# Low parts of weight chunks on a second engine in the mixer's input projection of a decoder step

## The chip, the cores and the metric

The kernel runs on one core of one Trainium2 chip. The metric is the device time of one launch in microseconds (us), the median of several runs. The engines are called by the profile's names: PE (TensorE, matrix products), DVE (VectorE), ACT (ScalarE), POOL (GpSimd) and SP (SyncE, which here only issues DMAs). SBUF is the on-chip memory that all of them read; PE writes its products to PSUM, from where DVE and ACT read them.

## The reference

One layer of a hybrid decoder is computed for 256 new prompt tokens and 8 sample tokens (264 columns in all), with 2048 features. Everything is fp32.

```
x = x + 0.5 * swiglu(rmsnorm(x, n1), f1g, f1u, f1d)          # FFN 1, inner width 5504
h = rmsnorm(x, nm);  proj = h @ w_in                          # 38 column tiles of 128
o_att  = attend(q, k, v, sinks)                               # sliding window, T5 bias, sinks
o_rwkv, shift, S = rwkv_time_mix(proj[..., ATT_COLS:], ...)   # 16 heads, matrix state 64 x 64
x = x + concat(o_att, o_rwkv) @ w_out
x = x + 0.5 * swiglu(rmsnorm(x, n2), f2g, f2u, f2d)          # FFN 2
y = rmsnorm(x, final_norm)
```

In the recurrence `S = S * exp(lw) + sa * (kk*a) + v * k` the state passes from token to token. The outputs are y, the new key and value windows, the new states S and the shift state (`shift`, the last token's projected columns, which the next step mixes in).

## The kernel before

**Weight products.** A weight matrix comes from HBM in chunks of four 128x128 blocks (128x512 elements). `chunk` loads one (`raw`, six buffers, issued by SP), ACT rounds it to the format that PE takes at full speed (`hi`, L132), and DVE subtracts the two for the rest (`lo`, the low part, L59 through the helper `tt`). `hi` and `lo` have four buffers each. `gemm` then makes three products of 128x264 for each block: hi with the activation's high part, hi with its low part, and lo with its high part, twelve for a chunk. They add up in a PSUM bank `acc`. A tile of the input projection (`win(t)`) takes four chunks.

**Stages.** FFN 1, the mixer, FFN 2. In both FFNs nearly all work is weight products. The mixer goes through 38 input tiles in this order: two tiles for the small projections (t = 0, 1), then four batches of two head pairs, three tiles for each pair (t = 2 to 25), four key and value tiles (26 to 29) and eight query tiles (30 to 37); then the output projection in three passes (`wout`).

**What runs beside it.** Each head pair spawns a task `prep` (decay, keys, products inside blocks of 64 tokens, `gm` and `bk` among its tiles, small `XD` vectors for the sample tokens); each batch spawns one `chain`: it solves a triangular system by 30 dependent steps on DVE (`st`, `Xt`, from L59), builds the transition products (`m<-kr,TT` on PE), copies them out of PSUM (`W` at L622, `uv` at L626), and carries the state through four blocks. `shifted` evicts a tile (`pj`), and POOL copies the last columns into `shc` (L412), the shift state. Query tiles spawn `attend`. The function `tick` advances every task by one step after each chunk, so that small matmuls lie between weight products.

**Order.** The program is written in this interleaved order, and the tile framework's scheduler then lays each engine's instructions down in an order of its own, by priorities and its own model of durations; `tc.high_priority()` marks chunks and evictions. On the chip each engine takes its own queue in order. The queue matters for what follows: an instruction that waits holds all behind it. DMA issues of ACT and SP stand in these queues too, so a store that waits for its data holds the casts behind it.

## Time and profile before

| | |
|---|---|
| median of 3 runs | 1959.75 us (1958.75 to 1960.01) |
| profiled execution | 1958.83 us |
| its span, first to last instruction | 1957.0 us |
| busy PE, PEld | 1940.1, 1922.1 us |
| busy DVE, ACT, POOL | 1313.1, 1036.4, 264.1 us |
| mean granted clock of PE | 0.998 |

The page lists busy time by engine. PEld is the loading of weights into PE, which overlaps its products. A busy PE is not PE at its peak: the ends of matmuls are modelled. The chain of waits goes back from the last instruction to whatever released each step, and so tells which engine set the pace at which time. A row of a timeline has the start in us, the duration in us, the engine, the line, the operation, output and inputs by tile names, shapes, and in brackets the idle time before it and who ended it. A row of the groups by line has the number of instructions (x), their busy us, the mean ns of one, and the idle us ahead of them by releaser. A row of busy time by stretch has the stretch, its length, busy us (and instructions) of PE, PEld, DVE, ACT and POOL, the granted clock, the DMA engines' busy share and GB/s.

### The profile page before, as it was taken

The page shows a single profiled execution, that of the slowest core. Times are in us where ns is not written, and L with a number is a line of the kernel's source. Part 1 is how long each engine was busy: PE and PEld are TensorE (multiplying, and loading weights), DVE is VectorE, ACT ScalarE, POOL GpSimd, SP SyncE. Part 2 cuts the span into 40 slices and gives each one's busy share as a digit, 9 for nine tenths or more (in the row PEclk, how much of TensorE's full clock was granted, in tenths as well). Part 3 has the DMA queues.
Part 4 walks back from the last instruction along what each step waited for, and adds up shares of the span by engine and source line. Part 5 has one row for each costly group of instructions (what it writes and reads, how often), then busy time and mean ns, then how long its engine had stood idle before and what let it go on. Part 6 is the DMA issues. An engine that isn't in the chain of part 4 may idle for free.

```text
span 1957.0 us, 45229 instructions
## 1 busy us (share of the span) xinstructions
PE 1940.1 (99%) x17011; PEld 1922.1 (98%) x17011; DVE 1313.1 (67%) x2591; ACT 1036.4 (53%) x2069; POOL 264.1 (13%) x382
## 2 busy tenths in 40 slices
PE   9999999999999999999999999999999999999998
PEld 9999999999999999999889999999999999999998
DVE  5865555655556567799988766766666666666665
ACT  5644444444444456665556755654444444444445
POOL 0401001010010122232210000210101001010012
PEclk9999999999999999999999999999999999999999
DMA  7666666666656567555455455566666666666654
GB/s 241 178 194 194 186 194 196 184 189 178 188 183 185 184 194 230 165 162 153 136 151 167 137 157 185 176 187 188 191 189 193 188 194 191 191 195 183 195 182 148
DMA packets 218875, 357.26 MB, mean 183 GB/s; under 512 B 33552, under 2 KB 72352, under 8 KB 218656
## 3 DMA queue, kind: packets, MB, share of 16 engines
q1 hardware_dynamic: 212144, 345.76, 59.4%
q10 hardware_dynamic: 6512, 8.61, 1.4%
q8 instruction: 133, 2.18, 0.4%
q14 instruction: 86, 0.70, 0.1%
HBM read 346.67 MB, written 9.69 MB: 182 GB/s over the span
## 4 chain that ended last, share of the span: by engine, by line
PE 95%; DVE 3%; DMA 1%; issue 1%; ACT 1%; SPq 0%; DVEq 0%; POOL 0%; ACTq 0%
PE acc L75 87%; PE m L75 7%; DVE lo L59 1%; DVE Xt L59 0%; DVE st L59 0%; DMA Xt<-sa 0%; DMA x<-in_x 0%; DMA raw<-in_win 0%; DVE y L59 0%; SPq L564 0%; DVE gm L59 0%; ACT t L69 0%; DMA sa<-gm 0%; PE m L782 0%; ACT BT L521 0%
## 5 line engine op out<-in xcount | busy, mean ns | idle before, releaser
L59 DVE TENSOR_TENSOR lo<-raw,hi 128x512 fp32r<-128x512 f32 (+1 forms) x1288 | 874.5, 683 | 511.0 <-ACT hi L132 489.8
L132 ACT CAST hi<-raw 128x512 fp32r<-128x512 f32 (+1 forms) x1288 | 777.0, 606 | 822.0 <-PE acc L75 741.5
L75 PE MATMUL acc<-x,hi 128*128 128x264 f32 x5034 | 932.7, 286 | 2.2 <-DVE o L62 1.2
L75 PEld LDWEIGHTS acc<-x,hi 128*128 128x128 f32 x5034 | 781.4, 189 | 5.8 <-ACT hi L132 2.4
L75 PE MATMUL acc<-x,lo 128*128 128x264 f32 x2517 | 719.8, 286 | 0.5 <-DVE lo L59 0.5
L75 PE MATMUL acc<-h,hi 128*128 128x264 f32 x2752 | 495.0, 284 | 0.0
L75 PEld LDWEIGHTS acc<-x,lo 128*128 128x128 f32 x2517 | 475.5, 189 | 2.9 <-DVE lo L59 1.3
L75 PEld LDWEIGHTS acc<-h,hi 128*128 128x128 f32 x2752 | 424.4, 189 | 0.0
L75 PE MATMUL acc<-h,lo 128*128 128x264 f32 x1376 | 387.8, 284 | 0.0
L75 PEld LDWEIGHTS acc<-h,lo 128*128 128x128 f32 x1376 | 259.2, 189 | 0.0
L59 POOL TENSOR_TENSOR t<-t,t 128x264 f32<-128x264 f32 x74 | 80.3, 1085 | 1095.9 <-DVE t L59 949.7
L75 PE MATMUL acc<-y,hi 128*128 128x264 f32 x648 | 122.7, 284 | 0.0
L75 PE MATMUL acc<-o,hi 128*128 128x264 f32 x648 | 120.1, 284 | 0.0
L75 PE MATMUL acc<-kv,hi 128*128 128x264 f32 x582 | 109.2, 284 | 0.0
L75 PEld LDWEIGHTS acc<-y,hi 128*128 128x128 f32 x648 | 101.2, 189 | 0.1
L75 PEld LDWEIGHTS acc<-o,hi 128*128 128x128 f32 x648 | 100.1, 189 | 0.0
L62 DVE SCALAR_TENSOR_TENSOR x<-acc,x 128x264 f32<-128x264 f32 x192 | 81.2, 427 | 24.5 <-PE acc L75 23.6
L75 PE MATMUL acc<-y,lo 128*128 128x264 f32 x324 | 92.0, 284 | 0.0
L75 PE MATMUL acc<-o,lo 128*128 128x264 f32 x324 | 92.0, 284 | 0.0
L75 PEld LDWEIGHTS acc<-kv,hi 128*128 128x128 f32 x582 | 90.0, 189 | 0.0
L59 DVE TENSOR_TENSOR t<-acc,t 128x264 f32<-128x264 f32 x156 | 67.4, 432 | 32.8 <-PE acc L75 32.8
L75 PE MATMUL acc<-kv,lo 128*128 128x264 f32 x291 | 82.7, 284 | 0.0
(280 smaller groups left out, 1534.9 us busy)
## 6 DMA issues: line engine op xcount, KB each, us to landing
raw<-in_gu SPq DMA_DIRECT2D x688, 256.0 KB, 3.4
raw<-in_dn SPq DMA_DIRECT2D x224, 256.0 KB, 2.9
raw<-in_win SPq DMA_DIRECT2D x152, 256.0 KB, 3.4
raw<-in_dn SPq DMA_DIRECT2D x160, 192.0 KB, 2.7
raw<-in_wout SPq DMA_DIRECT2D x64, 256.0 KB, 3.3
xsp<-x ACTq DMA_DIRECT2D x16, 132.0 KB, 3.6
x<-xsp SPq DMA_DIRECT2D x16, 132.0 KB, 4.0
ld<-in_sT SPq DMA_DIRECT2D x16, 128.0 KB, 3.7
```

What stands on the lines that cost most here:

```text
L59: return e.tensor_tensor(out=out, in0=a, in1=b, op=op)
L62: return V.scalar_tensor_tensor(out=out, in0=a, scalar=s, in1=b, op0=op0, op1=op1)
L75: return TE.matmul(out, lhsT, rhs, start=start, stop=stop, **k)
L132: A.copy(hi[:, :w], raw[:, :w])
```

## The change

Four things are changed.

- From input tile 14 on (24 of 38 tiles), the low part of every second chunk of a tile is subtracted on POOL instead of DVE: 48 instructions.
- In `chain`, the copies `W` (two a batch) and `uv` (four a batch) all go to ACT; before, DVE had half of each.
- The sample tokens' values `Ys[k][:, NP:T]` are copied from `XD` by POOL early in `chain`, instead of by ACT near its end (eight copies of 128x8).
- The store of the shift state `shc` is written into the program at the second query tile instead of behind the last batch's tiles.

```
+SHARE = 14
-        def gemm(ps, src, xs, step=None, rng=None, ahead=True, ready=None):
+        def gemm(ps, src, xs, step=None, rng=None, ahead=True, ready=None, share=False):
...
-                hi, lo = ready or chunk(src[:, k0 * P:k1 * P], k1 - k0, V, ahead)
+                hi, lo = ready or chunk(src[:, k0 * P:k1 * P], k1 - k0, G if share and k0 // CH % 2 else V, ahead)
...
-                gemm(ps, I["win"][t], n2.xs, tick)
+                gemm(ps, I["win"][t], n2.xs, tick, share=t >= SHARE)
...
                 Ys = [yb[bt.p0 + k] for k in range(n)]
+                for k in range(n):
+                    G.tensor_copy(Ys[k][:, NP:T], XD[:, 7, bt.p0 + k, :])
...
-                    (A.copy, V.tensor_copy)[k % 2](W[:, k], v[:, 1:4, 0:64])
+                    A.copy(W[:, k], v[:, 1:4, 0:64])
...
-                        (V.tensor_copy, A.copy)[h](uv[HALF[h], :, k, HALF[h]], v[HALF[h], :, 64:128])
+                        A.copy(uv[HALF[h], :, k, HALF[h]], v[HALF[h], :, 64:128])
...
-                    A.copy(Ys[k][:, NP:T], XD[:, 7, bt.p0 + k, :])
...
-                    if len(bat) == len(BATCH):
-                        A.dma_start(O["sh"], shc)
...
                 else:
+                    if i == 1:
+                        A.dma_start(O["sh"], shc)
                     ps = win(LKV + 4 + i)
```

## The prediction

> **What bounds the kernel now.** I read the page first, then the chain of waits, then busy time by stretch.

> ```profile
> span 1957.0 us, 45229 instructions
> PE 1940.1 (99%) x17011; PEld 1922.1 (98%) x17011; DVE 1313.1 (67%) x2591; ACT 1036.4 (53%) x2069; POOL 264.1 (13%) x382
> ...
> 65.80 691.23 PE acc L75 x5760
> ```

> The page makes TensorE (PE) look full everywhere. That is true of the two FFNs: the chain has 5760 weight products in a row, 691.23 / 5760 = 0.120 us each, with nothing between them. One weight chunk is 12 products, so PE needs 12 x 0.120 = 1.44 us for it. In the mixer the same 99% is misleading, because the modelled ends of matmuls cover their gaps. There I go by who leads the chain. The tiles that the change touches (14 to 37) run from the load in the first row below to the eviction of the last query tile in the second.

> ```profile
> 833.42 0.33 SPq L131 DMA_DIRECT2D raw<-in_win  x1
> ...
> 1066.88 0.43 DVE L62 SCALAR_TENSOR_TENSOR o<-acc,rs 128x264 f32<-128x264 f32 x1
> ```

> I cut these 234 us where the chain changes its leader. Busy time of PE, PEld, DVE, ACT, POOL in each piece:

> ```profile
> 833.00:861.00 28.00, 28.00 (x228) 27.70 (x227) 27.56 (x69) 18.78 (x48) 10.48 (x18) 1.00 0.60 182
> 861.00:879.00 18.00, 17.10 (x243) 16.11 (x243) 16.58 (x58) 11.96 (x36) 3.72 (x13) 1.00 0.50 133
> 879.00:932.00 53.00, 53.00 (x591) 50.75 (x584) 48.24 (x123) 32.83 (x74) 10.77 (x22) 1.00 0.54 152
> 932.00:960.00 28.00, 26.16 (x379) 23.88 (x379) 24.07 (x76) 15.69 (x44) 7.43 (x17) 1.00 0.55 150
> 960.00:989.00 29.00, 29.00 (x318) 27.62 (x315) 28.18 (x89) 17.72 (x39) 4.51 (x12) 1.00 0.43 124
> 989.00:1029.00 40.00, 37.47 (x545) 35.26 (x545) 31.11 (x93) 21.07 (x57) 6.18 (x16) 1.00 0.55 148
> 833.00:1067.00 234.00, 228.46 (x2647) 216.93 (x2647) 208.01 (x606) 142.00 (x358) 47.34 (x104) 1.00 0.53 150
> ```

> The chain's shares by line, first for 879 to 932, then for 989 to 1029, then for the whole 833 to 1067:

> ```profile
> by line: PE acc L75 73.4%; PE m L75 25.7%; PE m L474 1.1%
> by line: DVE lo L59 13.7%; PE acc L75 12.1%; DMA raw<-in_win 10.0%; DVE st L59 9.1%; DVE Xt L59 8.9%; issue 7.3%; SPq L564 5.9%; DMA Xt<-sa 5.5%; DVE t L442 4.3%; DMA sa<-gm 3.8%; DVE o L62 2.5%; DVE t L59 1.9%; DVE kr L59 1.6%; DVE uv L626
> by line: PE acc L75 49.6%; PE m L75 15.2%; DVE lo L59 5.0%; DVE Xt L59 3.5%; DVE st L59 3.4%; issue 3.2%; DMA Xt<-sa 2.7%; DMA raw<-in_win 1.7%; SPq L564 1.5%; DVE gm L59 1.4%; DMA sa<-gm 1.0%; ACT BT L521 0.9%; DVE t L59 0.8%; ACT kr L512
> ```

> So PE leads some pieces wholly (100% in 879 to 932) and others hardly at all (12.1% in 989 to 1029). Over the whole, 64.8% is PE; about a third of 234 us, some 80 us, is led by something else, and VectorE (DVE) is most of that. DVE is busy 208.01 of 234 us, and in the PE-led pieces before each gap it is at 91 to 98%, so its backlog is carried into the next gap. DVE work taken out of a PE-led piece therefore still counts, one piece later. That holds until 1029; behind it PE leads again, and I give relief there no value.

> **The parts, one by one.** Groups by line, DVE and ACT; the first three rows are for 833 to 1067, the others for 757 to 1205:

> ```profile
> L59 DVE TENSOR_TENSOR lo<-raw,hi 128x512 fp32r<-128x512 f32 x105 | 71.2, 683 | 6.3 <-ACT hi L132 5.1 <-PE acc L75 0.7
> L59 DVE TENSOR_TENSOR Xt<-Xt,st 128x60 f32<-128x60 f32 (+10 forms) x120 | 24.6, 205 | 2.3
> L59 DVE TENSOR_TENSOR st<-X,Xt 128x60 f32<-128x60 f32 (+10 forms) x120 | 24.5, 204 | 4.7 <-DMA Xt<-sa 2.9
> ...
> L626 DVE COPY uv<-m 64x256 f32<-64x256 f32 x8 | 3.3, 407 | 0.0
> L622 DVE COPY W<-m 128x192 f32<-128x192 f32 x4 | 1.4, 343 | 0.0
> L626 ACT COPY uv<-m 64x256 f32<-64x256 f32 x8 | 2.9, 368 | 3.4 <-DVE uv L626 3.2
> L680 ACT COPY y<-XD 128x8 f32<-128x8 f32 x8 | 1.6, 197 | 5.5 <-POOL XD L59 5.5
> ```

> *Low parts to GpSimd.* 24 tiles x 2 chunks = 48 subtractions leave DVE. What matters is DVE's work up to the point where PE, which takes its instructions in order, needs a batch's transition product. In the order in which the instructions are laid down, the first such product of the four batches stands behind 75.9, 106.3, 133.6 and 153.1 input chunks before, and behind 73.8, 100.7, 127.6 and 147.0 after: the scheduler moves them forward. I take the third, the last ahead of 1029. Tile 14 starts at chunk 56. Before, DVE makes 133.6 - 56 = 77.6 low parts up to there; after, 71.6 chunks come first, and half of them, 35.8, are DVE's. Saved: 41.8 x 0.683 = 28.5 us.

> *Copies to ScalarE.* Two batches' copies lie ahead of that point: 4 uv x 0.407 + 2 W x 0.343 = 2.3 us off DVE. ACT gains 12 copies at about 0.37 and loses 8 y copies x 0.197, +2.9 us in all, and is busy 142.00 of 234 us; a batch's six copies now stand one behind the other on one engine, but DVE's half had ACT waiting 3.2 us already. I put this at nothing; without that cover it is at most 3 us. The y copies move to GpSimd behind the XD values they read, so ACT's 5.5 us of waiting goes; the casts behind it have a ring of four pairs, so nothing for that either.

> *Forward move.* Six chunks fewer in front of the product are six more behind it, where PE leads: 6.0 x 1.44 = 8.6 us that DVE must first earn.

> *The price on GpSimd.* No row shows a 512-wide subtraction there. Nearest are these; POOL and DVE as they meet in the first FFN, then in the dense part:

> ```profile
> 302.68 1.20 POOL L59 TENSOR_TENSOR t<-t,t 128x264 f32<-128x264 f32 x1 [8.89 <-DVE t L59]
> 302.56 0.69 DVE L59 TENSOR_TENSOR lo<-raw,hi 128x512 fp32r<-128x512 f32 x1
> ...
> 856.27 2.67 POOL L468 COPY XD<-t 128x8 f32<-128x8 f32 x2 [1.43 <-DVE t L62]
> 856.27 0.68 DVE L59 TENSOR_TENSOR lo<-raw,hi 128x512 fp32r<-128x512 f32 x1
> ...
> 858.68 0.42 DVE L59 TENSOR_TENSOR pj<-acc,rs 128x264 f32<-128x264 f32 x1
> ...
> 1059.81 0.76 POOL L59 TENSOR_TENSOR x<-y,x 128x264 fp32r<-128x264 f32 x1 [0.89 <-ACT x L921]
> 1060.25 0.87 DVE L59 TENSOR_TENSOR lo<-raw,hi 128x512 fp32r<-128x512 f32 x1
> ```

> At 302.68 GpSimd's 264 columns end at 303.88, and DVE's subtraction ended at 303.25: 0.63 us once DVE had finished, so 512 columns should take 0.63 x 512 / 264 = 1.22 us (an estimate). At 856.27 two copies of 8 columns take 2.67 us, because they sit until DVE, after a run of work on two SBUF inputs, reaches pj, which reads PSUM. At 1060.25 it is DVE that is held: 0.87 instead of 0.69. So the two engines exclude each other when both read SBUF this way. [...]

> What DVE loses for each of the 35.8: the bound below is 0 (GpSimd runs while DVE is idle or reads PSUM), the bound above the full 1.22 us. [...] The three SBUF groups above, 71.2 + 24.6 + 24.5 = 120.3 us, fill 51% of the 234 us. 0.8 x 0.51 = 0.41 us; smaller such groups push it up, the 48 subtractions gone push it down. 35.8 x 0.41 = 14.7 us.

> *Shift state.* ACT's queue, the ACT copy behind it, and PE's wait for that copy:

> ```profile
> 953.75 0.35 ACTq L887 DMA_DIRECT2D out_sh<-shc  x1
> 954.14 0.75 ACT L609 COPY TT<-m 32x256 f32<-32x256 f32 x2 [3.83 <-POOL shc L412]
> ...
> PE m L75 <- ACT TT L609: 1.5, 1, 1.5
> ```

> In the changed order the store still stands between the same two chunks' casts and still waits for the last shc copy on GpSimd, but the TT copy is now ahead of it. PE's 1.5 us may go; casts now stand behind the store instead. I take 1.0 of gain, between 1.5 and nothing.

> **The sum.** 28.5 + 2.3 - 14.7 = 16.1 us of DVE relief, less 8.6 = 7.5, plus 1.0 = 8.5 us. The profiled execution took 1958.83 us (span 1957.0 and 1.8 around it), 0.9 below the median of 1959.75. 1958.83 - 8.5 = 1950.3, in terms of the median 1951.

> **Rivals.** [...] Price: if each GpSimd subtraction blocks DVE for 0.95 us, 35.8 x 0.95 = 34 against 30.8 saved, and PE, sent six chunks early to a product that isn't ready, loses 3.2 + 8.6 = 11.8: 1970.6, or 1971.5 by the median. It decides from (30.8 - 8.6) / 35.8 = 0.62 us of blocking. For it: the 2.67 us row. Against: reciprocals and PSUM readers are spread through the same pieces, and GpSimd is let in at those. [...]

> A cast, for the second rival:

> ```profile
> 939.41 0.62 ACT L132 CAST hi<-raw 128x512 fp32r<-128x512 f32 x1
> ```

> *No change: late low parts eat the gain.* A GpSimd subtraction that first sits out a run of 2.5 us and then takes 1.22 comes 3.7 us after its cast. Four hi/lo pairs leave 3 x 1.44 - 0.62 = 3.7 us. So the slack is just used up; some eight such cases of 1 us each would leave nothing of 8.5: 1959. For it: GpSimd's queue also holds shc and XD copies that wait for DVE. Against: it is empty 187 of 234 us.

> *Much faster: GpSimd runs in DVE's shadow.* Blocking of 0.05 us: 30.8 - 1.8 - 8.6 + 1.5 = 21.9, 1937, by the median 1938. For it: DVE idles more once relieved. Against: the three rows above. That the scheduler leaves the work where it was is ruled out: 48 subtractions stand in GpSimd's queue.

> **Chances.** A measurement of this kernel can tell about 0.2%, 3.9 us, from no change. The forecast and its surroundings (blocking 0.2 to 0.55) get 0.48, much faster 0.14, no change 0.14, slower 0.24. So faster 0.62, same 0.14, slower 0.24. The range goes from the much-faster case, 1938, to just short of the slower case's middle, 1969.

> **What would show it.** Right: GpSimd's lo near 1.2 to 1.5 us, longer in dense pieces; DVE's busy time between 833 and the end of the input tiles down by some 20 us net; the chain in the three gaps shorter, and the share of PE in it above 64.8%; the FFNs unchanged at 0.120 us a product. Wrong, slower: DVE's st, Xt and remaining lo visibly longer than 204, 205 and 683 ns, GpSimd's lo above 2 us, and "POOL lo" in the chain. The forecast falls if DVE's remaining low parts grow past 0.9 us, or if GpSimd's lo take the place of DVE's in front of PE.

## The result and the profile after

The changed kernel takes **1978.8 us** (median of 4 runs, 1977.23 to 1979.46) where the kernel before, run beside it, takes 1959.88 us (4 runs, 1958.75 to 1960.69): a ratio of 1.0096, 95% interval 1.0078 to 1.0113. It is slower by 18.9 us. The forecast was 1951.0, the range ended at 1969: the direction was wrong, and the time lies between the slower rival at its price of 0.95 us (1971.5) and what the same sum gives at the full 1.22 us for each subtraction (35.8 x 1.22 - 30.8 + 8.6 = 21.5 us, so 1981).

The profiled execution took 1979.46 us, 1958.83 before. The head of its page, then the two FFNs in the chain of waits, before and after (start, length, what):

```profile
span 1977.5 us, 45234 instructions
PE 1948.9 (99%) x17011; PEld 1928.8 (98%) x17011; DVE 1315.3 (67%) x2531; ACT 1039.8 (53%) x2073; POOL 313.3 (16%) x438
```

```profile
65.80 691.23 PE acc L75 x5760
...
1259.62 685.48 PE acc L75 x5712
```

```profile
65.75 691.23 PE acc L76 x5760
...
1280.09 685.48 PE acc L76 x5712
```

Both FFNs are what they were, 691.23 and 685.48 us. The second one starts 1280.09 - 1259.62 = 20.5 us later, and the span is 1977.5 - 1957.0 = 20.5 us longer. So all of it lies in the mixer. Busy time there in the stretch that the prediction used, the last query tile's eviction and the busy time up to it, and the chain's shares for the first row:

```profile
833.00:1067.00 234.00, 216.76 (x2433) 203.75 (x2431) 196.66 (x516) 130.81 (x327) 88.41 (x149) 0.97 0.48 133
...
1103.49 0.43 DVE L63 SCALAR_TENSOR_TENSOR o<-acc,rs 128x264 f32<-128x264 f32 x1
...
833.00:1104.00 271.00, 253.76 (x2882) 238.35 (x2881) 218.38 (x593) 156.92 (x405) 96.65 (x160) 0.97 0.48 134
```

```profile
by line: PE acc L76 35.5%; PE m L76 14.9%; DVE Xt L60 6.9%; DVE lo L60 6.6%; DVE st L60 6.0%; issue 5.5%; DMA raw<-in_win 2.1%; DVE t L60 2.0%; DVE t L63 1.9%; DVE gm L60 1.6%; DVE bk L60 1.4%; DMA sa<-gm 1.1%; DMA ld<-in_bias 1.1%; DMA Xt<
```

In the same 234 us PE gets 2433 recorded instructions done instead of 2647, and its idle time is 234 - 216.76 = 17.2 us instead of 5.5. Its granted clock is 0.97 instead of 1.00. POOL's busy time rose by 41 us. DVE's reads 196.66 instead of 208.01, but these 234 us hold less of the work: the input tiles now end at 1103.9 us instead of 1067.3, and up to there DVE is busy 218.38 us. Over the whole execution it executes 60 instructions fewer (2531 for 2591, by the pages) and is busy 1315.3 us where it was 1313.1. So the relief that the prediction expected, some 20 us, did not show in DVE's busy time at all. PE's share of the chain is 50.4%, where the prediction had "above 64.8%" as the sign of being right. The groups by line for the first 234 us show what took the relief's place:

```profile
L60 POOL TENSOR_TENSOR lo<-raw,hi 128x512 fp32r<-128x512 f32 x44 | 57.9, 1315 | 54.9 <-ACT hi L133 49.5 <-PE m L76 2.9 <-issue 2.0
...
L60 DVE TENSOR_TENSOR lo<-raw,hi 128x512 fp32r<-128x512 f32 x50 | 38.4, 768 | 10.3 <-ACT hi L133 10.2
L60 DVE TENSOR_TENSOR Xt<-Xt,st 128x60 f32<-128x60 f32 (+10 forms) x120 | 35.2, 293 | 2.7
L60 DVE TENSOR_TENSOR st<-X,Xt 128x60 f32<-128x60 f32 (+10 forms) x120 | 30.8, 257 | 8.2 <-DMA Xt<-sa 5.7
...
L63 DVE SCALAR_TENSOR_TENSOR t<-pj,nmu,t 128x264 f32<-128x264 f32 x15 | 9.5, 637 | 2.6 <-ACT t L415 2.3 <-ACT t L70 0.4
...
L60 DVE TENSOR_TENSOR gm<-m,C 128x512 f32<-128x512 f32 x12 | 7.8, 680 | 0.0
...
L60 DVE TENSOR_TENSOR pj<-acc,rs 128x264 f32<-128x264 f32 x15 | 6.3, 417 | 0.1
```

POOL's subtraction takes 1.315 us, close to the 1.22 that was estimated. On DVE, what works on two SBUF inputs grew: `lo` from 683 to 768 ns, `Xt` from 205 to 293, `st` from 204 to 257, `t` (L63) from 482 to 637. What reads PSUM did not: `gm` has 680, `pj` 417 (685 and 422 before). That was the prediction's sign for "wrong, slower"; of its other two, GpSimd's `lo` above 2 us did not come, and "POOL lo" led the chain for one piece of 1.30 us only, at 970.45 us. The view of one tile shows that this isn't a general slowing. Behind the count it has minimum, median and maximum in ns; before and then after:

```profile
L59 DVE TENSOR_TENSOR Xt<-Xt,st x120: 149/208/278, 843.6 to 1038.0; 128x60 f32<-128x60 f32 x16, 128x28 f32<-128x28 f32 x8, 128x48 f32<-128x48 f32 x8, 128x42 f32<-128x42 f32 x8
```

```profile
L60 DVE TENSOR_TENSOR Xt<-Xt,st x120: 159/210/1306, 843.9 to 1039.1; 128x60 f32<-128x60 f32 x16, 128x28 f32<-128x28 f32 x8, 128x48 f32<-128x48 f32 x8, 128x42 f32<-128x42 f32 x8
```

The median stands (208 to 210); the longest grew from 278 to 1306 ns, the length of one whole POOL subtraction. One such meeting in the timeline:

```profile
1002.32 0.19 DVE L60 TENSOR_TENSOR st<-X,Xt 128x28 f32<-128x28 f32 x1
1002.48 1.26 POOL L60 TENSOR_TENSOR lo<-raw,hi 128x512 fp32r<-128x512 f32 x1 [0.48 <-PE m L76]
1002.54 1.25 DVE L60 TENSOR_TENSOR Xt<-Xt,st 128x28 f32<-128x28 f32 x1
1003.72 0.68 DVE L60 TENSOR_TENSOR lo<-raw,hi 128x512 fp32r<-128x512 f32 x1
```

`Xt` on 28 columns is issued 0.06 us after POOL's `lo`, should take some 0.2 us, and ends at 1003.79, just behind POOL at 1003.74. It waited out the whole POOL instruction.

PE's waits between 833 and 1205 (total, times, longest) have changed in kind. Before, the longest was the 1.5 us on `ACT TT` that the prediction quotes:

```profile
PE m L76 <- ACT TT L610: 4.5, 1, 4.5
PE m L76 <- DVE st L60: 3.3, 1, 3.3
PE m L734 <- ACT t L486: 2.3, 1, 2.3
PE m L510 <- ACT t L486: 2.3, 1, 2.3
PE m L510 <- DVE gm L60: 2.1, 2, 1.9
...
PE acc L76 <- POOL lo L60: 0.6, 1, 0.6
```

Four of these five are followed by something that the profile before does not have. Three stretches around the last of them, at 868 us:

```profile
868.00:871.00 3.00, 1.12 (x11) 0.87 (x8) 2.90 (x8) 2.21 (x9) 0.71 (x1) 1.00 0.18 49
871.20:874.60 3.40, 3.40 (x38) 3.16 (x38) 3.12 (x14) 2.27 (x7) 0.00 (x0) 0.50 0.17 28
874.70:878.00 3.30, 3.30 (x85) 3.28 (x84) 3.03 (x13) 1.44 (x5) 2.03 (x6) 1.00 0.86 226
```

PE is idle for 3.0 - 1.12 = 1.9 us, and then its granted clock is 0.50 for 3.4 us, and 1.00 again. The timeline of PE shows what that does: three products start in 0.36 us ahead of it and in 0.66 us inside it (start, duration):

```profile
866.03 0.40 PE L76 MATMUL acc<-x,hi 128*128 128x264 f32 x2
...
866.39 0.40 PE L76 MATMUL acc<-x,hi 128*128 128x264 f32 x2
...
872.12 0.64 PE L76 MATMUL acc<-x,hi 128*128 128x264 f32 x2
...
872.78 0.64 PE L76 MATMUL acc<-x,hi 128*128 128x264 f32 x2
```

There are five such stretches of 3.41 us in this execution, from 871.2, 939.4, 1024.8, 1038.4 and 1093.0 us; the first four begin within 1.5 us of the end of a gap of 1.9 to 4.5 us between two of PE's products. The profiled execution before has none up to its last product.

**Bookkeeping.** PE's idle time (span less busy PE, from the pages) grew from 1957.0 - 1940.1 = 16.9 us to 1977.5 - 1948.9 = 28.6 us: 11.7 us. A stretch of 3.41 us at half clock costs up to 1.7 us while PE has work: five make 8.5. Together 20.2 of the 20.5 us. So the loss in this execution is waits of PE, and then a slow clock that some of them bring with them. Five stretches against none overstates the clock's part between the medians: the profiled execution of the kernel before has a mean clock of 0.998, and of 65 runs of that kernel beside the experiments only 22 have it. Their mean is 0.9969, that of the changed kernel's four runs 0.9938; 0.0031 of some 1970 us is 6 us at most (an estimate).

### The profile page after: what moved, and what is told of

Its sections match the earlier page's. It is cut to its first block, busy times and chain, and to the rows that moved or that the text cites. A ratio compares the mean times of both kernels' runs of the same rounds, so it can differ in the third digit from the quotient of the medians.

```text
span 1977.5 us, 45234 instructions
## 1 busy us (share of the span) xinstructions
PE 1948.9 (99%) x17011; PEld 1928.8 (98%) x17011; DVE 1315.3 (67%) x2531; ACT 1039.8 (53%) x2073; POOL 313.3 (16%) x438
## 4 chain that ended last, share of the span: by engine, by line
PE 93%; DVE 4%; DMA 1%; issue 1%; SPq 0%; ACT 0%; POOL 0%; DVEq 0%; ACTq 0%
PE acc L76 85%; PE m L76 7%; DVE lo L60 1%; DVE Xt L60 1%; DVE st L60 1%; DMA raw<-in_win 0%; DVE y L60 0%; DVE t L60 0%; DVE t L63 0%; DMA x<-xsp 0%; DMA x<-in_x 0%; DVE t L718 0%; DVE gm L60 0%; DVE bk L60 0%; PE m L517 0%
## 5 line engine op out<-in xcount | busy, mean ns | idle before, releaser
L60 DVE TENSOR_TENSOR lo<-raw,hi 128x512 fp32r<-128x512 f32 x1240 | 847.8, 687 | 520.7 <-ACT hi L133 499.2
L63 DVE SCALAR_TENSOR_TENSOR x<-acc,x 128x264 f32<-128x264 f32 x192 | 81.1, 427 | 24.5 <-PE acc L76 23.6
```

What stands on the lines that cost most here:

```text
L60: return e.tensor_tensor(out=out, in0=a, in1=b, op=op)
L63: return V.scalar_tensor_tensor(out=out, in0=a, scalar=s, in1=b, op0=op0, op1=op1)
```

## The experiments

The theory behind the result was that **the exclusion** decides: a POOL subtraction and DVE's work on two SBUF inputs exclude each other, as in the rows at 1002 us. The expectations call it the ports; the runs show the exclusion and its price, and not what in the chip makes it. Rivals: **late low parts** (POOL is merely slow, so PE waits for `lo`), **the other three edits**, and **no headroom** (relieving DVE was never worth what I put on it). "Before" in each result is the unchanged kernel on the same chip; the difference is between medians, the interval that of the ratio.

**e1, the low parts alone.** Only the first of the four edits:

```
+SHARE = 14
...
+    hi, lo = ready or chunk(src[:, k0 * P:k1 * P], k1 - k0, G if share and k0 // CH % 2 else V, ahead)
...
+    gemm(ps, I["win"][t], n2.xs, tick, share=t >= SHARE)
```

> Only the low parts go to GpSimd; the copies, the sample values and the store stay as before. All three theories (the shared ports, late low parts, the forward move in PE's order) put the loss into this part: 1975 to 1983 us, with PE's clock halved for 3.4 us in some places as in the changed kernel. If the loss came from the six copies now in a row on ACT, or from the store, it would be near 1960.

Measured 1975.89 us against 1960.31: +15.6, ratio 1.0078 [1.0064, 1.0092]. The low parts alone make most of the loss.

**e2, the rest alone.** The other three edits, with all low parts on DVE:

```
-    gemm(ps, I["win"][t], n2.xs, tick, share=t >= SHARE)
+    gemm(ps, I["win"][t], n2.xs, tick)
```

> The three other edits without the low parts. All three theories: 1955 to 1961 us, DVE relieved by 4.7 us and nothing on the ports. If ACT's copies in a row cost 3 us a batch, it would be 1965 or more.

Measured 1967.37 against 1960.31: +7.1, 1.0036 [1.0022, 1.0050]. The part that I had put "at nothing" costs as well. 15.6 + 7.1 = 22.7, and the whole change costs 18.9; each of the three has an interval of some 3 us to either side, so the two parts add up within it.

**e3, the subtraction twice.** DVE keeps all low parts; POOL repeats 48 of them into a tile that nobody reads. So PE and DVE lose nothing and wait for nothing, and only the meeting is added:

```
+    tt(V, lo[:, :w], raw[:, :w], hi[:, :w].bitcast(F32), ALU.subtract)
+    if e is G:
...
+        tt(G, two[:, :w], raw[:, :w], hi[:, :w].bitcast(F32), ALU.subtract)
```

> The kernel before, DVE making every low part as before; in the same 48 chunks GpSimd makes the same subtraction once more into a tile that nobody reads. Nobody waits for GpSimd's result and DVE is relieved of nothing; PE's order is that of before to within 0.2 chunks at the transition products. Ports: DVE's work from 833 us on stretches by about 0.6 us for each of the 48, some 25 to 30 us, and the time rises by 10 to 35 us. Late low parts: nobody waits, 1960 +- 2. Forward move: no forward move, 1960 +- 2.

Measured 1991.23 against 1960.31: **+30.9 us, 0.64 us for each of the 48**, 1.0155 [1.0141, 1.0169]. No product hangs on POOL's results here, so late low parts cannot be the cause. POOL also holds `raw` and `hi` until it has read them, but ACT's casts wait 0.6 us in all for it, and no wait of PE between 833 and 1205 us is for a cast. The groups of DVE and POOL between 833 and 1067 show the same stretching as in the changed kernel:

```profile
L60 DVE TENSOR_TENSOR lo<-raw,hi 128x512 fp32r<-128x512 f32 x92 | 68.8, 751 | 3.2 <-ACT hi L133 3.2
L60 POOL TENSOR_TENSOR two<-raw,hi 128x512 fp32r<-128x512 f32 x43 | 63.3, 1474 | 42.4 <-ACT hi L133 33.4 <-ACT t L489 3.7 <-issue 3.6
...
L60 DVE TENSOR_TENSOR st<-X,Xt 128x60 f32<-128x60 f32 (+10 forms) x119 | 36.7, 309 | 4.4 <-DMA Xt<-sa 2.5
L60 DVE TENSOR_TENSOR Xt<-Xt,st 128x60 f32<-128x60 f32 (+10 forms) x118 | 33.3, 282 | 2.2
```

**e4, no reading on POOL.** The changed kernel, but POOL writes zeros twice instead of subtracting, so it reads no SBUF (the low parts of these 48 chunks are missing from its result):

```
+    if e is G:
+        for _ in range(2):
+            G.memset(lo[:, :w].bitcast(F32), 0.0)
...
```

> The changed kernel, but GpSimd writes zeros twice into the low tile instead of subtracting, so it reads nothing from SBUF (the low parts of these 48 chunks are left out of the result). PE's order is that of the changed kernel to within 0.7 chunks, the work moved off DVE the same. Ports: DVE's st and Xt stay at 204 and 205 ns, and the time falls below before, 1935 to 1952. Forward move: PE is sent forward as in the changed kernel, 1965 to 1980. Late low parts: the zeros do not wait for the cast, so this theory too expects no loss; e3 tells it from the ports.

Measured 1957.26 against 1960.31: -3.1, 0.9983 [0.9974, 0.9992]. Taking POOL's SBUF inputs away takes 1978.8 to 1957.3, and DVE's busy time from 1315.3 to 1287.9 us. The zeros don't wait for the cast either, so e4 alone would not tell the exclusion from late low parts; e3 does, and e5 excludes POOL's work as such. Together the three show the exclusion. What is left, with the copies' price in it (e6), is a gain of 3 us, where the prediction's sum without blocking, 30.8 - 8.6 + 1.0, has 23.

**e5, POOL busy, nothing taken off DVE.** Before, plus two memsets of a tile of POOL's own in each of the 48 chunks:

```
+    for _ in range(2):
...
+        behind(G.memset(two, 0.0))
```

> As e3 (the kernel before, 48 extra pieces of work on GpSimd that nobody waits for), but each is two memsets of a tile of its own, which read nothing from SBUF. Ports: DVE's st and Xt stay at 204 and 205 ns, 1960 +- 2. If GpSimd's work as such (its queue, its writes) were the cost in e3, this would be 1975 or more.

Measured 1960.05 against 1959.72: +0.3, 1.0003 [0.9994, 1.0012]. DVE's groups and POOL's, as for e3:

```profile
L60 DVE TENSOR_TENSOR lo<-raw,hi 128x512 fp32r<-128x512 f32 x104 | 70.8, 686 | 7.4 <-ACT hi L133 6.5 <-PE acc L76 0.3
...
L138 POOL MEMSET two<- 128x512 f32 x96 | 46.7, 523 | 0.2
L60 DVE TENSOR_TENSOR st<-X,Xt 128x60 f32<-128x60 f32 (+10 forms) x120 | 24.8, 207 | 6.5 <-DMA Xt<-sa 4.7
L60 DVE TENSOR_TENSOR Xt<-Xt,st 128x60 f32<-128x60 f32 (+10 forms) x120 | 24.6, 205 | 2.2
```

`lo`, `st` and `Xt` stand at 686, 207 and 205 ns beside 46.7 us of memsets on POOL. The memsets cost nothing that can be told (+0.3 us); 48 subtractions of two SBUF inputs cost 30.9 us in e3.

**e6, the copies alone.** Before, with all `W` and `uv` copies on ACT:

```
-    (A.copy, V.tensor_copy)[k % 2](W[:, k], v[:, 1:4, 0:64])
+    A.copy(W[:, k], v[:, 1:4, 0:64])
...
-    (V.tensor_copy, A.copy)[h](uv[HALF[h], :, k, HALF[h]], v[HALF[h], :, 64:128])
+    A.copy(uv[HALF[h], :, k, HALF[h]], v[HALF[h], :, 64:128])
```

> Of the three edits in e2, the copies to ACT alone. PE's order has the third and fourth batch's transition products at 132.2 and 148.6 chunks, as in e2 (before: 133.6 and 153.1). Forward move: the loss of e2 is here, 1964 to 1970, with waits of about 3 us and a halved clock near 995 and 1030 us. If the loss of e2 came from the values on GpSimd or the store: 1957 to 1961.

Measured 1966.84 against 1959.72: +7.1, 1.0034 [1.0022, 1.0047]: all of e2. PE's waits name two places, near 1030 and 996 us; behind each come 3.4 us of half clock (from 1031.9 and 997.8):

```profile
PE m L75 <- DVE st L59: 3.5, 1, 3.5
PE acc L75 <- DVE o L62: 2.7, 1, 2.7
```

**e7, the fourth batch held back.** The copies of e6, with the fourth batch's transition products 14 steps later:

```
+    yield from pause((0, 0, 0, 14)[bt.i])
```

> e6 with the fourth batch's task held back by 14 steps ahead of its transition product, which puts that product at 154.2 chunks (before 153.1, e6 148.6); the third stays at 132.2. Forward move of the fourth batch: back to 1958 to 1963. If ACT's six copies in a row are the cost: as e6.

Measured 1965.32 against 1959.72: +5.6, 1.0031 [1.0019, 1.0042]. Its two long waits are the same (3.6 and 2.7 us): the fourth batch's place is not the main cause; the 1.5 us between e6 and e7 lie within the intervals.

**e8, values and store alone.** The y copies on POOL and the later store of the shift state:

```
+    G.tensor_copy(Ys[k][:, NP:T], XD[:, 7, bt.p0 + k, :])
...
-    A.copy(Ys[k][:, NP:T], XD[:, 7, bt.p0 + k, :])
...
-    A.dma_start(O["sh"], shc)
...
+    A.dma_start(O["sh"], shc)
```

> The other two edits of e2 without the copies: the sample values on GpSimd and the store written later. PE's transition products stand where they stood before. Forward move: 1957 to 1961. If these two are the cost of e2: 1964 to 1970.

Measured 1960.29 against 1959.72: +0.6, 1.0001 [0.9992, 1.0010]. Nothing, as the prediction had it for the values; of the 1.0 us for the store nothing is seen.

**e9, the relief alone.** Before, with the 48 low parts taken off DVE and zeros written on POOL in their place, and the copies left as they were:

```
+    if e is G:
+        for _ in range(2):
+            G.memset(lo[:, :w].bitcast(F32), 0.0)
...
```

> The kernel before with the one thing that e4 had: in 48 chunks GpSimd writes zeros twice instead of DVE subtracting (those low parts are left out of the result). [...] This is what the relief of DVE is worth at most, whatever engine took the work. By the sum on record, in which DVE's time counts one for one less 8.6 us for the forward move: 1960 - 24 = 1936. By e2 and e4 (1967 to 1957): 1950 +- 3.

Measured 1953.13 against 1960.66: **-7.5 us**, 0.9967 [0.9955, 0.9979]. 48 x 0.683 = 32.8 us of DVE instructions went, POOL read no SBUF in their place, and the kernel gained 7.5. DVE's busy time on the page fell by 23.0 us only, from 1313.1 to 1290.1: where neighbouring instructions overlap, it counts that time once (in the rows at 1002 us, `lo` starts at 1003.72 and `Xt` ends at 1003.79). Busy time and the chain's shares for 833 to 1067:

```profile
833.00:1067.00 234.00, 232.60 (x2799) 220.97 (x2797) 188.78 (x582) 146.92 (x380) 80.26 (x200) 1.00 0.52 146
```

```profile
by line: PE acc L76 61.6%; PE m L76 29.7%; PE m L521 1.1%; DMA Xt<-sa 1.1%; DVE st L60 0.9%; SPq L569 0.7%; DVE Xt L60 0.7%; PE m L479 0.7%; PE m L514 0.6%; DVE lo L60 0.6%; issue 0.5%; PE m L737 0.2%; POOL t L60 0.2%; ACT kr L534 0.2%; PE 
```

DVE fell to 188.78 us and PE's share of the chain rose to over 91%. PE's idle time in the stretch is 1.4 us. Before it was 5.5; there was not much more to be had. The third batch's first transition product, the prediction's point of reckoning, before and in e9:

```profile
1018.91 1.31 PE L75 MATMUL m<-kr,TT 64*64 64x128 f32 x20
...
1006.96 2.18 PE L76 MATMUL m<-kr,TT 64*64 64x128 f32 x32
```

It comes 11.9 us earlier, and 4.6 input chunks that stood ahead of it now stand behind it (129.0 instead of 133.6), which is 6.6 us of PE at 1.44 us each. So the 7.5 us already hold a forward move.

**e10, copies on both.** ACT makes all copies, DVE repeats its old half into an unread tile:

```
+    V.tensor_copy(ring((P, 256), "two", 1)[:, :192].rearrange("p (c t) -> p c t", c=3), v[:, 1:4, 0:64])
```

> ACT makes all six copies of a batch in a row, as in e6, but DVE also makes its old half once more into a tile that nobody reads, so DVE is relieved of nothing and PE's order stays near that of before (transition products at 75.9, 107.1, 133.5 and 153.1 chunks). If ACT's copies in a row are the cost of e6: 1965 to 1969. If the moved order is: 1958 to 1962.

Measured 1966.05 against 1960.66: +5.4, 1.0034 [1.0022, 1.0047]. That is in the range set for ACT's row of copies, and PE waits 3.4 us near 1025 us for ACT's `TT`, with the third batch's transition product within 0.1 chunks of its old place. But later products of the first two batches stand up to 2.8 chunks later than before, so the order on PE moved here too, and the run doesn't decide.

**e11, every fourth chunk.** 24 POOL subtractions instead of 48, nothing else:

```
+    G if share and k0 // CH == 1 else V
```

> As e1, but one chunk in four instead of one in two goes to GpSimd: 24 subtractions. By e1 (+15.6 for 48) and a price that is the same for each: +8, 1968 +- 3. If the loss came only where subtractions come close together: less than +4.

Measured 1967.96 against 1960.66: +7.3, 1.0039 [1.0026, 1.0053], about half of e1. Neither of the two doses does good: 0.30 and 0.32 us net for each.

**e12, the chain ahead on DVE.** Before, with the two DVE steps between the transition products put ahead in the scheduler:

```
+    with tc.high_priority():
         tt(V, N, pN[:, :n * 256].rearrange("p (k c t) -> p k c t", k=n, c=4),
...
```

> The kernel before with two of the chain's DVE steps (the sum into kr and the product N) at high priority, so that they stand ahead of the next batch's st and Xt steps in DVE's queue. In the trace of before N stood some 3 us behind its inputs there. If that wait sets PE's pace: 1954 to 1958, faster than both kernels. If PE has other work meanwhile: 1958 to 1962.

Measured 1959.86 against 1960.66: -0.8, 0.9999 [0.9990, 1.0007]. No gain.

**e13, e14, e15, which copies.** Only the four `W` copies to ACT; only the eight `uv` copies; and the opposite of e6, all copies on DVE:

```
+    A.copy(W[:, k], v[:, 1:4, 0:64])                                # e13
+    A.copy(uv[HALF[h], :, k, HALF[h]], v[HALF[h], :, 64:128])       # e14
+    V.tensor_copy(W[:, k], v[:, 1:4, 0:64])                         # e15
+    V.tensor_copy(uv[HALF[h], :, k, HALF[h]], v[HALF[h], :, 64:128])
```

> Before with only the four W copies of DVE moved to ACT (uv stays split). Theory A, ACT's row of copies is the price (6.5 us for twelve copies moved): a third of it, +2 us. Theory B, the order on PE is the price: here too the scheduler lays the third batch's first state products 1.8 input chunks earlier (26.1 instead of 24.3 chunks ahead of the last input chunk), so the whole +6.5 us. Theory C, scatter of the granted clock alone: within 1 us of before.

> Before with only the eight uv copies of DVE moved to ACT (W stays split). Theory A: two thirds of 6.5 us, +4.3 us. Theory B: the third batch's products come 1.5 chunks earlier on PE, +6.5 us. Theory C: within 1 us of before.

> The opposite of e6: all W and uv copies on DVE, none on ACT; third batch's products 0.4 chunks earlier than before. Theory A with its mirror, a row of six copies on one engine is the price wherever it stands: +6.5 us or more, since DVE is fuller than ACT. Theory B: nearly nothing from the order, and DVE gets 12 x 0.39 = 4.7 us more work, of which the relief run says about a quarter counts, so +1 us. Theory C: within 1 us of before.

Measured 1970.83, 1970.02 and 1970.22 against 1960.71: +10.1, +9.3 and +9.5; ratios 1.0049 [1.0036, 1.0061], 1.0047 [1.0035, 1.0059], 1.0049 [1.0036, 1.0062]. Four copies cost as much as twelve, so a price for each copy on ACT (theory A) falls. PE's waits of e13, e14 and e15:

```profile
PE m L75 <- ACT W L622: 3.5, 1, 3.5
```

```profile
PE m L75 <- DVE W L622: 3.5, 1, 3.5
PE acc L75 <- DVE o L62: 2.8, 1, 2.8
```

```profile
PE m L75 <- ACT TT L609: 4.4, 1, 4.4
```

In e13 and e14, as in e6, PE waits 3.5 us near 1027 us, in the third batch's state products, which the scheduler has laid 1.4 to 1.8 chunks (2.0 to 2.6 us) earlier in PE's queue; the operand it waits for has another name each time. That speaks for theory B. But e15 kept the third batch within 0.4 chunks, for which theory B had +1 us, and lost 9.5: there the 4.4 us wait stands near 952, in the second batch, on ACT's `TT`. So with each of these divisions some state product stands in PE's queue 3.5 to 4.4 us ahead of its operand; which product it is differs. That the order on PE alone makes the loss is not shown: no kernel was run with the copies moved and PE's queue held as it was. What makes the copies' 7 us stays open.

**The bookkeeping over the runs.** The same two terms as for the changed kernel, from each profiled execution: the change of PE's idle time (span less busy PE, 16.9 us before), and 1.7 us for each 3.41 us at half clock ahead of the second FFN's end.

| run | PE idle | half clock | sum | span |
|---|---|---|---|---|
| whole change | +11.7 | 5 x 1.7 = 8.5 | +20.2 | +20.5 |
| e1, low parts | +11.8 | 3 x 1.7 = 5.1 | +16.9 | +17.6 |
| e3, twice | +21.4 | 3 x 1.7 = 5.1 | +26.5 | +31.9 |
| e4, no reading | -3.2 | 1 x 1.7 | -1.5 | -3.4 |
| e6, copies | +4.0 | 4 x 1.7 = 6.8 | +10.8 | +8.9 |
| e9, relief | -4.5 | none | -4.5 | -6.3 |
| e11, 24 of 48 | +3.6 | 2 x 1.7 = 3.4 | +7.0 | +8.7 |
| e13, `W` | +4.8 | 5 x 1.7 = 8.5 | +13.3 | +14.9 |
| e15, DVE | +7.6 | 3 x 1.7 = 5.1 | +12.7 | +11.3 |

But for e3 the two terms give the span within 2 us, in the seven runs that aren't in the table too. The rest of a span's change is that of busy PE by definition, so the table tests the second term only: the half clock accounts for nearly all the growth of busy PE. None of the kernels that compute everything was faster than before beyond the noise.

## Why the prediction was wrong

**The step that failed first: what relief of DVE is worth.** The prediction took the share of the chain not led by PE, "some 80 us", for time that DVE's relief could win back, one for one, and called the busy PE misleading. e9 measures that step alone, with the forward move that comes with it. By the prediction's way of counting, DVE has 129.0 - 56 = 73.0 chunks ahead of the third batch's product there, 36.5 of them its own, and saves (77.6 - 36.5) x 0.683 = 28.1 us up to it; the product came 11.9 us earlier. Taken with the forward move, the sum on record made 24 us of it; 7.5 were won, 0.16 us for each subtraction. The term 28.5 + 2.3 = 30.8 us was too large by more than half. One reason is in the rows: it charged DVE 0.683 us for each subtraction, while its busy time fell by 23.0 us for 48, 0.48 each. A second is argued and not shown: the chain names the last releaser of each step, and where DVE leads, a path through PE may be only a little shorter. A nearer measure stood in the same quoted row: PE busy 228.46 of 234 us, so 5.5 us of visible idle time there and little behind it. With e9's 7.5 in place of 30.8 - 8.6 and its own 14.7 of blocking, the same sum is a loss of 6 us: 7.5 - 14.7 + 1.0.

**The price of the exclusion: that DVE is held was right, the size too small.** It took 0.41 us of blocking for each POOL subtraction, 0.8 us times the share (51%) of DVE's SBUF groups. No run shows the 0.8 us; it was an estimate, the estimated 1.22 us of a POOL subtraction less the 0.42 us of `pj`. What the runs show is a loss of up to a whole POOL instruction in single meetings, 1.25 us for an `Xt` of 0.2 us, and a mean of about half of the 1.22. From the groups after, `lo` 50 x 0.085, `Xt` 120 x 0.088, `st` 120 x 0.053 and `t` at L63 15 x 0.155 make 23.5 us for the 44 subtractions in the stretch, 0.53 us each, and the groups shown are not all. As time it is 0.46 us each by the changed kernel against e4 (18.9 + 3.1 = 22.0 us), 0.48 by e1 against e9 (15.6 + 7.5 = 23.1 us) and 0.64 in e3, where DVE keeps all its work. The slower rival said that blocking decides from 0.62 us; the point lay lower, since its sum held 30.8 us of relief. The share of 51% is an average; that POOL's `lo` comes just where DVE is in a row of `st` and `Xt`, all of which read two SBUF inputs, is argued from rows like those at 1002 us and not counted.

**The copies "at nothing; at most 3 us": wrong.** 7.1 us (e6), above the bound. Their durations were not the matter: four copies cost as much as twelve. State products then stand in PE's queue where their operands aren't ready, and the longest single wait grows from 1.5 to 3.4 us or more; why is open.

**The forward move.** Put at 8.6 us for the third batch with low parts and copies together. e7, which takes the fourth batch's move back, wins 1.5 us of the copies' 7.1, within the noise. The third batch's move was not tested by itself.

**Not foreseen: the clock.** The prediction priced a wait of PE at its own length. In the changed kernel four of the five gaps of 1.9 us or more were followed by 3.41 us at half clock, up to 1.7 us on top of each; with a fifth stretch that no gap explains, 8.5 of the 20.5 us in the profiled execution, less between the medians (at most 6 us, the estimate above). It has nothing for this among its terms or rivals.

**Right.** The duration of POOL's subtraction (1.22 estimated, 1.26 to 1.315 measured); the exclusion and whom it hits (SBUF readers, not `gm` or `pj`); FFNs unchanged; nothing for the values. Of its signs for "right" only the FFNs' and the duration came: DVE's busy time did not fall, and PE's share of the chain did. The rival of late low parts is excluded by e3 and e5: PE waits 0.6 us in all for POOL's `lo` in the changed kernel.

## What to carry to other kernels

Before counting on relief of an engine, look at the idle time of the engine that bounds the kernel: it is a nearer measure of the gain (here 5.5 us in the stretch, for 7.5 won) than the share of the chain that other engines lead. Compare busy time over the same work and not over the same microseconds: in a fixed window DVE seemed relieved by 11 us, over the whole execution by nothing. A task handed to GpSimd that read two SBUF inputs had a price on VectorE's two-input work here, 0.46 to 0.64 us of time for each 512-column subtraction, where its relief won 0.16; test it by letting GpSimd repeat the work into an unread tile. And in this kernel, whose longest wait of TensorE between 833 and 1205 us was 1.5 us, moving even cheap copies between engines left a product 3.4 us or more ahead of its operand (e6, e7, e10, e13 to e15); look at the longest single waits of TensorE, not at the durations moved.

## What the runs showed of the hardware

**Half clock after short gaps.** Gaps of 1.9, 2.3, 3.3 and 4.5 us in the changed kernel, and of 1.5 us in e5, e12, e13 and e14, were followed within 1.5 us of their end by a granted clock of 0.50 for 3.413 us. The gap's length alone doesn't decide: the same gap of 1.5 us stands in the execution before and in e8 without effect, 2.3 us from 1003.0 us in the changed kernel brought none, and 2.8 us on `o` in e14 brought none. What tells most of the cases apart is how much of the idle time falls into one step of a grid. In the changed kernel and in e6 the changes of the clock lie whole multiples of 3.413 us from one another: the five stretches of the changed kernel start 20, 25, 4 and 16 such steps apart, those of e6 from 997.8, 1031.9 and 1144.6 us 10 and 33. The steps just ahead of the changed kernel's first four stretches have 1.88, 1.96, 2.70 and 3.01 us of idle PE; the two that share its gap of 2.3 us have 1.33 and 1.20. Three steps of e14, two that share the gap of 2.8 us and one with a gap of 3.5 us, behind which the half clock starts at 1027.7 us:

```profile
993.60:997.00 3.40, 2.06 (x18) 1.85 (x16) 3.35 (x6) 1.68 (x3) 0.00 (x0) 1.00 0.39 136
997.00:1000.40 3.40, 1.93 (x16) 1.96 (x17) 3.34 (x8) 0.89 (x2) 1.30 (x2) 1.00 0.58 137
1024.30:1027.70 3.40, 0.67 (x22) 0.67 (x24) 3.19 (x14) 0.67 (x2) 0.66 (x1) 1.00 0.57 169
```

**The scatter of one kernel goes with the clock.** Of the runs of the kernel before, 6 with a mean clock of 0.995 have a mean of 1962.4 us, and 22 with 0.998 have 1959.2 us: about 1 us for each 0.001.

**GpSimd beside VectorE, by kind of work.** 96 memsets of 512 columns (523 ns each) changed nothing on VectorE (e5: `lo`, `st` and `Xt` at 686, 207 and 205 ns, 683, 204 and 205 before); 48 subtractions of two SBUF inputs cost 31 us (e3).

**Products on rounded and on fp32 operands.** In the kernel before, weight products on the rounded `hi` and `lo` start 0.120 us apart with 264 columns; two products `m<-kv,o` on fp32 operands, at 1060.45 and 1060.66 us, start 0.21 us apart with 256.
